# A hybrid RWKV-7 / sparse-attention layer on one core: block 1's weight sums of the feed-forward moved from accumulating transfers to VectorE, and the fp32r weight parts moved to other offsets

## The chip, the cores and the metric

One core of a Trainium2 chip runs the whole kernel. The metric is the device time of one execution in microseconds (us), as a median over runs. A profiled execution gives a trace beside it: when each instruction began on each engine, and what it waited for. The engines are PE (TensorE: matmuls, and PEld, its weight loads), DVE (VectorE), ACT (ScalarE), POOL (GpSimd) and SP (SyncE, which issues most of the DMA transfers here).

## What is computed

One layer for 512 tokens of width 1024 in float32. A normalised input is multiplied by one wide matrix `w_in`; its columns feed an RWKV-7 group (a recurrence, solved in chunks) and a sparse-attention group; both results go through `w_out`. Then comes the part that the change is mostly about, a SwiGLU feed-forward of inner width 2816, and a last norm:

```python
h = h + jnp.concatenate([y_r, y_n], axis=-1) @ w_out[l]
xn = rms_norm(h, norm_ffn[l])
h = h + (jax.nn.silu(xn @ w_gate[l]) * (xn @ w_up[l])) @ w_down[l]
return rms_norm(h, norm_final)
```

## The kernel before, in words

**Products in three matmuls.** A float32 product is made of fp32r parts: each operand is split into a high half (ACT copies it with rounding, L145) and a low half (DVE subtracts the high half from the value, L147). `mm3` (L163 to L166) then adds up three matmuls: high by high (L164), high by low (L165), low by high (L166). For each matmul PE loads a *stationary* operand of 128 columns and streams a *moving* operand of 256 or 512 columns past it; the load for the next matmul runs while the present one streams. L164 and L165 of a product differ in one operand only.

**Gate and up.** The 2816 inner columns are done in 11 blocks of 256 (`q` = 0 to 10). A block is a Strassen-like scheme: a 2 by 2 split of (w_gate, w_up) against a 2 by 2 split of the tokens takes seven products instead of eight, named by their weights: B11, B21, T2, T1, T3, B22, T4. Each product (`prod`) is 24 matmuls of 128x256: 2 halves of 128 columns, 4 blocks of the inner dimension, three matmuls each. The weights' parts are stationary; the tokens' parts (A11, A12, S1 to S4, A22) are made once, and move. Four raw quarters of a block come from memory: B11 and B21 (w_gate), B12 and B22 (w_up). The sums are T1 = B11 + B12, T2 = T1 + B22, T3 = B12 + B22 and T4 = T2 + B21.

**How the sums are made** (`class Weights`). `load_rest` issues on SP a plain transfer of B11 into the tile `t1` (L1154), of B22 into `b22` (L1155) and of B12 into `t3` (L1156). POOL then issues two transfers that *add* into what lies there: B12 onto `t1` (L1158) and B22 onto `t3` (L1159). So T1 and T3 come out of memory transfers, each a plain one and an adding one behind it. DVE makes T2 (L1163) and T4 (L1171). `put` splits each weight into its parts.

**Block 1 and the handover.** Blocks 0 and 1 are prepared while `w_out` is multiplied and the tokens' parts are made (`ffn_norm`). Block 0's sums are early. Block 1's `t1`, `t2` and `t3` lie in a tile of the tag `L`, which comes free only when the token parts have been made from the tile `raw` (last read at L1090 and L1114). The trace shows block 1's transfers as `L<-in_w_gate_dram` and `L<-in_w_up_dram`.

**The order of the work** is set by a scheduler at build time that places each engine's instructions in one fixed row, by its own estimate and by `tc.high_priority()`. Each engine works its row in order.

**Where the parts lie.** `parts` and `operand` cut the parts out of tiles that have 64 spare elements, from element `off` on (4 bytes each). The start addresses in a partition, mod 256, in the program as built: the tiles `whi` and `wlo` at 160; `L` (A11, A12, S3, A22; xh, xl) at 160; `gin` (S2) and `b8` (S4) at 32; `kB` (S1) at 64; the window operand `t4` of `job_cmp1` at 160. So a weight part in gate and up (off=56, 224 bytes) lies at 128, and a part that moves in the projections (off=8, 32 bytes; `moving` lists those jobs) at 192. Block 0's B11, B21, T2 and T1 lie in `b8` tiles without an offset.

Of the kernel before, what the change touches and what calls it, by code (L numbers as in the profile page):

```python
# [46 lines left out]
def hybrid_layer(ctx: ExitStack, tc: tile.TileContext, x, positions, norm_mix, w_in, mu_shift, w0, w2, a0, a2,  # L47
                 g2, k_k, k_a, r_k, lnx_w, lnx_b, pe_k, wk1, bk1, wk2, pe_v, wv1, bv1, wv2, w_out, norm_ffn,
                 w_gate, w_up, w_down, norm_final, out):
    nc = tc.nc  # L50
    PE, DVE, ACT, POOL = nc.tensor, nc.vector, nc.scalar, nc.gpsimd
# [12 lines left out]
    def st(shape, tag, bufs=1, dtype=F32):  # L64
        return sb.tile(list(shape), dtype, name=tag, tag=tag, bufs=SB_BUFS.get(tag, bufs))
# [3 lines left out]
    w_in, w_out, w_gate, w_up, w_down = (w.rearrange("l a b -> (l a) b") for w in (w_in, w_out, w_gate, w_up, w_down))  # L69
# [22 lines left out]
    raw0 = st([128, 2048], "wraw").rearrange("p (k n) -> p k n", n=256)  # L92
# [48 lines left out]
    def split(src, hi, lo, pool=False, lo_pool=False):  # L141
        if pool:
            POOL.tensor_copy(hi, src)
        else:
            ACT.activation(hi, src, AF.Copy)  # L145
        pool = pool or lo_pool
        (POOL if pool else DVE).tensor_sub(lo, src, hi.bitcast(F32))  # L147

    def parts(raw, tags=("whi", "wlo"), pool=False, lo_pool=False, off=0):

        b, n = raw.shape[1:]
        hi, lo = (st([128, 2048 + PAD], tag, 2, F32R) for tag in tags)
        v = [t[:, off:off + b * n].rearrange("p (k n) -> p k n", n=n) for t in (hi, lo)]
        with tc.high_priority():
            for k in range(0, b, max(b // 2, 1)):
                e = k + max(b // 2, 1)
                split(raw[:, k:e], v[0][:, k:e], v[1][:, k:e], pool, lo_pool)
        return v
# [58 lines left out]
    def proj_tok(w, t, m=1):  # L217

        n = w[0].shape[2]
        p = pj()  # L220
        for u in range(m):
            sl = slice((t + u) * 128, (t + u + 1) * 128)
            for k in range(KB):
                mm3(p[:, u * n:u * n + n], xh[:, k, sl], xl[:, k, sl], w[0][:, k], w[1][:, k], k == 0, k == KB - 1)
        return p[:, 0:m * n]
# [74 lines left out]
    for t in range(NT):  # L300
        next(norm)
        if t == 0:
            w0p = parts(raw0, off=8)
        ACT.activation(ctok[:, t].rearrange("p h d -> p (h d)"), proj_tok(w0p, t), AF.Copy)
    w1p = parts(raw1, lo_pool=True)
    pt = ps("s")
# [193 lines left out]
    def job_r(half):  # L500
        def f(w):
            if "rar" not in T:
                T["rar"] = st([128, 4, 2, S], "L")
            for j in range(2):
                i = half * 2 + j
                rx = st([128, S], "t2")
                mix(proj_tile(w, j * 128), i, rx)
                DVE.tensor_mul(ch(T["rar"][:, i, 1]), ch(rx), T["ep"][:, i, :, 1:65])
        return f
# [79 lines left out]
    def job_v(half):  # L589
        def f(w):  # L590
            if half == 0:
                T["rv"] = st([128, 4, S], "b8")
            for j in range(2):
                i = half * 2 + j
                mix(proj_tile(w, j * 128), 8 + i, T["rv"][:, i])
        return f
# [48 lines left out]
    def job_qs(half):  # L645
        def f(w):
            if half == 0:
                T["qtok"] = st([128, NT, 8, 64], "b8")
            for t in (0, 2):
                rotate(T["qtok"][:, t:t + 2, 4 * half:4 * half + 4], tok_pair(w, t), tab_pair(t), 0.125)  # L650
        return f
# [70 lines left out]
    def cols(c0, n=256):  # L722
        return lambda: load(w_in[:, c0:c0 + n], n)
# [11 lines left out]
    def load_kv(c):  # L735
        raw = st([128, 2048], "wraw").rearrange("p (k n) -> p k n", n=256)
        for b in range(2):
            c0 = kvw + 256 + c + 256 * b
            nc.sync.dma_start(raw[:, :, b * 128:b * 128 + 128], w_in[:, c0:c0 + 128].rearrange("(k p) n -> p k n", p=128))
        return raw  # L740

    mk, mv = cmp_jobs(wk1, 0), cmp_jobs(wv1, 1)
    def then(job, *fs):
        return job[0], lambda w: [f(w) if f is job[1] else f() for f in (job[1],) + fs]

    hk, hv = lambda: hidden(0, "bk1"), lambda: hidden(1, "bv1")
    jobs = [(None, job_lat), (load_tail, job_tail), (cols(1024), job_v(0)), mk[0], then((cols(1280), job_v(1)), gate), mk[1], then((cols(512), job_k(0)), hk), mv[0], (cols(768), job_k(1)), then(mv[1], hv), then((cols(0), job_r(0)), solve, compressed), (cols(256), job_r(1)), then((lambda: load_kv(128), job_vt), solve2), (lambda: load_kv(0), job_ks), then((cols(RCOLS), job_qs(0)), solve3, solve4), (cols(RCOLS + 256), job_qs(1))]

    moving = [jobs[i][1] for i in (3, 5, 7, 9, 12, 13, 14, 15)]
    raws, w = [jobs[1][0]()], w1p  # L750
    for n, (_, f) in enumerate(jobs):
        if n + 2 < len(jobs):
            raws.append(jobs[n + 2][0]())
        wn = parts(raws.pop(0), off=8 if jobs[n + 1][1] in moving else 0) if raws else None
        f(w)
        w = wn

# [187 lines left out]
    for t in range(NT):  # L945
        n = (t + 1) * 128
# [120 lines left out]
    def operand(tag, off=0):  # L1067
        v = st([128, 2048 + (PAD if tag in ("whi", "wlo") else 0)], tag, dtype=F32R)[:, off:off + 2048]
        v = v.rearrange("p (x k n) -> p x k n", x=2, n=256)
        return v[:, 0], v[:, 1]  # L1070
# [6 lines left out]
    def ffn_norm(src):  # L1077
        xn2 = st([128, 2, D], "b8")
        for t in range(NT):
# [36 lines left out]
                put("A22", a22)  # L1116
            yield

    turn2 = [0]

    class Weights:
# [12 lines left out]
        def put(self, name, v, tag=None):  # L1134
            if tag is None:
                tag = ("whi", "wlo")[turn2[0] % 2]
                turn2[0] += 1
            o = operand(tag, 56 if tag != "b8" else 0)
            split(v, *o)
            setattr(self, name, o)  # L1140

# [5 lines left out]
        def load_rest(self):  # L1147
            self.b22 = st([128, 2048], "wraw")[:, 0:1024].rearrange("p (k n) -> p k n", n=256)
            if self.q % 2:
                tt = st([128, 4, HK, 256], "L")  # L1150
                self.t1, self.t2, self.t3 = (tt[:, i] for i in range(3))
            else:
                self.t1, self.t2, self.t3 = (st([128, HK, 256], "t4") for _ in range(3))
            nc.sync.dma_start(self.t1, self.quarter(w_gate, 0))  # L1154
            nc.sync.dma_start(self.b22, self.quarter(w_up, 1))  # L1155
            nc.sync.dma_start(self.t3, self.quarter(w_up, 0))  # L1156
            with tc.high_priority():
                POOL.dma_start(self.t1, self.quarter(w_up, 0), accum_op=OP.add)  # L1158
                POOL.dma_start(self.t3, self.quarter(w_up, 1), accum_op=OP.add)  # L1159

        def middle(self, tag=None):
            with tc.high_priority():
                DVE.tensor_add(self.t2, self.t1, self.b22)  # L1163
                self.put("T2", self.t2, tag)
                self.put("T1", self.t1, tag)

        def end(self):
            with tc.high_priority():
                self.put("T3", self.t3)
                self.put("B22", self.b22)  # L1170
                DVE.tensor_add(self.t2, self.t2, self.b21)  # L1171
                self.put("T4", self.t2)
# [135 lines left out]
    for n, (a, b) in enumerate(GROUPS):  # L1308
        one, two = halves[n]
        a11, a21, a12, a22 = (h[:, :, x] for h in (one, two) for x in (left, right))  # L1310
        lead, end = n == 0, n == 1
        t1, t2 = block4(a, 0, "wraw"), block4(b, 1, ("gin", "kB")[n])
        t3 = st([128, 4, 512], "wraw") if lead else None
        t3 = [t3[:, 2 * i:2 * i + 2] if lead else st([128, 2, 512], "t4") for i in range(2)]
        for i in range(2):
            nc.sync.dma_start(t3[i], down(a, 1)[:, 2 * i:2 * i + 2])
        t2s.append(t2)
        DVE.tensor_sub(a21, a22, a21)
        multiply(m1, a_side(a11), b_side(t1), lead, end)
        DVE.tensor_add(a11, a21, a11)  # L1320
        with tc.high_priority():
            for i in range(2):
                h = slice(2 * i, 2 * i + 2)
                DVE.tensor_add(t1[:, h], t1[:, h], t3[i])
                POOL.dma_start(t3[i], down(b, 1)[:, h], accum_op=OP.add)
            DVE.tensor_add(t2, t2, t1)
        multiply(m5, a_side(a21), b_side(t1), lead, end)
        multiply(m6, a_side(a11), b_side(t2), lead, end)
        DVE.tensor_sub(a21, a11, a22)
        multiply(m7, a_side(a21), b_side(t3), lead, end)  # L1330
# [30 lines left out]
    for t, banks in accumulate(*jit(lambda k: hid[PLAIN[k]]), w_down, 6, None, [PLAIN[k] * 128 for k in (0, 2, 4)], held, rest):  # L1361
        xo, o = x2[:, t], o2[:, t % 2]
# [49 lines left out]
```

## Time and profile before

| | |
|---|---|
| median of 3 runs | 751.76 us (751.45 to 752.36) |
| the profiled execution, device time | 753.52 us |
| its span, first to last instruction | 751.5 us |
| PE / DVE / ACT / POOL busy | 720.7 / 592.5 / 399.6 / 165.1 us |
| mean granted TensorE clock | 0.979 |

The profiled execution took 1.76 us more than the median of the runs, and 2.0 us of it lie around the span. Times in the trace count from the span's start. A matmul's duration in the trace overlaps that of the next one, so what a matmul costs in a row of matmuls is read from start to start. The gate and up blocks stand between about 413 and 634 us; the `w_in` projections between 11 and 212 us; the down projection follows up to the end.

### The profile page before, as it was taken

Reading aid. Unit: us, or ns where it says so; the run is one execution under the profiler, and the core shown is the slowest. Engines: PE = TensorE matmul, PEld = TensorE weight load, DVE = VectorE, ACT = ScalarE, POOL = GpSimd, SP = SyncE. Lnnn points to the kernel's source line nnn. Section 1 sums busy time; section 2 is a strip of 40 time slices with the busy share of each in tenths; the row PEclk is TensorE's granted clock in tenths of the full one; section 3 lists DMA queues with packets and bytes.
Section 4 is the critical chain, followed back from the end, with each engine's and each line's share of the span. In section 5 each row is a group of like instructions: output and inputs, shape, how many; then the busy total and the mean of one; then the engine's idle time right before and its main releaser. Section 6 shows DMA issues by size and latency. Waiting matters only on the chain.

```text
span 751.5 us, 14937 instructions
## 1 busy us (share of the span) xinstructions
PE 720.7 (96%) x6045; PEld 630.3 (84%) x6045; DVE 592.5 (79%) x1089; ACT 399.6 (53%) x666; POOL 165.1 (22%) x262
## 2 busy tenths in 40 slices
PE   7999999998889999999999969999999999999996
PEld 6867887898778788767788969999999999877885
DVE  5488688879868888788358959869798899999835
ACT  6398735324367866757538535435444455465414
POOL 3210053038534452443000111111101101010000
PEclk8999999999989999999999979999999999999998
DMA  7723543100062000230320778887867719453302
GB/s 252 206 82 110 168 113 112 57 3 2 3 222 33 2 2 2 57 115 1 113 85 1 190 159 227 184 221 169 225 168 187 180 57 287 161 113 112 141 0 112
DMA packets 73466, 87.01 MB, mean 116 GB/s; under 512 B 4996, under 2 KB 62934, under 8 KB 73398
## 3 DMA queue, kind: packets, MB, share of 16 engines
q1 hardware_dynamic: 60694, 72.43, 29.4%
q0 software_dynamic: 12704, 13.63, 11.8%
q8 instruction: 47, 0.77, 0.4%
q14 instruction: 21, 0.17, 0.1%
HBM read 83.96 MB, written 2.10 MB: 115 GB/s over the span
## 4 chain that ended last, share of the span: by engine, by line
PE 66%; DVE 23%; DMA 5%; issue 3%; ACT 2%; POOL 0%; SPq 0%; DVEq 0%; ACTq 0%
PE ps_ra L166 6%; PE ps_ra L165 6%; PE ps_ra L164 6%; PE ps_pj L166 6%; PE ps_pj L164 5%; PE ps_pj L165 5%; PE ps_o L1006 3%; DVE wlo L147 3%; PE ps_s L166 3%; PE ps_s L164 3%; PE ps_s L165 3%; DMA L<-in_w_up_dram 3%; PE ps_pj L998 3%; DVE L L147 2%; DVE whi L147 2%
## 5 line engine op out<-in xcount | busy, mean ns | idle before, releaser
L145 ACT ACTIVATE whi<-wraw 128x1024 fp32r<-128x1024 f32 (+1 forms) x63 | 62.7, 1032 | 40.7 <-issue 11.7
L147 DVE TENSOR_TENSOR wlo<-wraw,whi 128x1024 fp32r<-128x1024 f32 (+1 forms) x46 | 58.4, 1295 | 15.6 <-ACT whi L145 12.1
L995 POOL TENSOR_SCALAR whi<-whi,m,gates 128x128 f32<-128x128 f32 (+3 forms) x64 | 42.5, 680 | 37.2 <-DVE m L993 28.7
L166 PE MATMUL ps_ra<-L,wlo 128*128 128x512 f32 (+2 forms) x136 | 48.0, 354 | 0.0
L165 PE MATMUL ps_pj<-L,whi 128*128 128x512 f32 (+1 forms) x128 | 45.2, 353 | 0.0
L164 PE MATMUL ps_pj<-L,whi 128*128 128x512 f32 (+1 forms) x128 | 44.8, 355 | 0.3 <-ACT whi L145 0.3
L165 PE MATMUL ps_ra<-L,whi 128*128 128x512 f32 (+2 forms) x128 | 44.1, 345 | 0.0
L166 PE MATMUL ps_pj<-L,wlo 128*128 128x512 f32 (+1 forms) x128 | 43.9, 343 | 0.1
L164 PE MATMUL ps_ra<-L,whi 128*128 128x512 f32 (+2 forms) x128 | 43.8, 344 | 0.0
L992 ACT ACTIVATE whi<-whi,m 128x128 f32<-128x128 f32 (+3 forms) x64 | 35.4, 554 | 9.6 <-DVE m L991 8.4
L164 PE MATMUL ps_ra<-whi,L 128*128 128x256 f32 (+1 forms) x108 | 34.4, 321 | 0.5 <-ACT L L145 0.5
L165 PE MATMUL ps_ra<-wlo,L 128*128 128x256 f32 (+1 forms) x108 | 34.5, 319 | 0.2 <-DVE wlo L147 0.2
L166 PE MATMUL ps_ra<-whi,L 128*128 128x256 f32 (+1 forms) x108 | 34.0, 316 | 0.0
L991 DVE CUSTOM_DVE_ANT_0 whi<-ps_s,negb 128x128 f32<-128x128 f32 (+3 forms) x64 | 29.3, 484 | 5.9 <-PE ps_pj L998 2.5
L166 PE MATMUL ps_pj<-whi,L 128*128 128x256 f32 (+1 forms) x108 | 33.8, 314 | 0.0
L165 PE MATMUL ps_pj<-wlo,L 128*128 128x256 f32 (+1 forms) x108 | 33.6, 312 | 0.0
L164 PE MATMUL ps_pj<-whi,L 128*128 128x256 f32 (+1 forms) x108 | 33.5, 313 | 0.0
L1158 POOL DMA_DIRECT2D t<-in_w_up_dram x6 | 8.0, 1332 | 97.6 <-DVE b L1090 58.0
L166 PEld LDWEIGHTS ps_ra<-L,wlo 128*128 128x128 f32 (+1 forms) x136 | 25.1, 185 | 4.0 <-issue 0.5
L166 PEld LDWEIGHTS ps_pj<-L,wlo 128*128 128x128 f32 x128 | 24.5, 191 | 3.7 <-DVE wlo L147 0.9
L164 PEld LDWEIGHTS ps_pj<-L,whi 128*128 128x128 f32 x128 | 24.4, 190 | 3.8 <-ACT whi L145 0.8
L165 PEld LDWEIGHTS ps_pj<-L,whi 128*128 128x128 f32 x128 | 24.4, 190 | 3.5 <-DVE L L147 0.4
(706 smaller groups left out, 2562.4 us busy)
## 6 DMA issues: line engine op xcount, KB each, us to landing
wraw<-in_w_gate_dram SPq DMA_DIRECT2D x22, 512.0 KB
wraw<-in_w_in_dram SPq DMA_DIRECT2D x9, 1024.0 KB
wraw<-in_w_down_dram SPq DMA_DIRECT2D x9, 1024.0 KB
t<-in_w_up_dram POOLq DMA_DIRECT2D x12, 512.0 KB, 6.5
wraw<-in_w_up_dram SPq DMA_DIRECT2D x11, 512.0 KB
L<-in_w_up_dram POOLq DMA_DIRECT2D x10, 512.0 KB, 6.0
wraw<-in_w_out_dram SPq DMA_DIRECT2D x4, 1024.0 KB
wraw<-in_w_in_dram SPq DMA_DIRECT2D x6, 512.0 KB
```

The lines of the kernel that those rows point to most:

```text
L145: ACT.activation(hi, src, AF.Copy)
L147: (POOL if pool else DVE).tensor_sub(lo, src, hi.bitcast(F32))
L164: PE.matmul(o, lh, rh, start=start, stop=False)
L165: PE.matmul(o, lh, rl, start=False, stop=False)
L166: PE.matmul(o, ll, rh, start=False, stop=stop)
L991: DVE.tensor_tensor_reduce(pr[:, i], pS[:, i], negb[:, S - n:S], scale=-1.0, scalar=3e38, op0=OP.add, op1=OP.min, accum_out=m[:, i, 0:1])
L992: ACT.activation(pr[:, i], pr[:, i], AF.Exp, scale=-1.0, bias=m[:, i, 0:1], accum_out=m[:, i, 1:2])
L995: POOL.tensor_scalar(pr[:, i], pr[:, i], m[:, i, 2:3], gv[:, 1 + b0 + i, h:h + 1], op0=OP.mult, op1=OP.mult)
L998: PE.transpose(pT[:, j], prr[:, x, j * 128:j * 128 + 128], ident)
L1006: PE.matmul(po[q, 2 * g:2 * g + 2], vtok[:, j % (t + 1), b0 + j // (t + 1), g], pTs[:, par, j], start=False, stop=g == 1 and bs[-1] == 1 a ...
L1158: POOL.dma_start(self.t1, self.quarter(w_up, 0), accum_op=OP.add)
```

## The change

Two things, in one diff:

1. For block 1 alone (`self.q == 1`) SP issues two plain transfers only: B12 into `t3` and B22 into `b22`. The plain transfer of B11 into `t1` and both adding transfers are gone. DVE makes T1 from the raw B11 (which is in SBUF for its own product anyway) and `t3`, then T2 as before, and T3 as `t3 + b22`.
2. The parts of weights get other offsets. In gate and up the offset depends on the product (`SHIFT`, elements), in the projections' moving weights it is 48 elements in place of 8.

```diff
@@ main loop over t (projection of the first columns)
-            w0p = parts(raw0, off=8)
+            w0p = parts(raw0, off=48)
@@ loop over jobs
-        wn = parts(raws.pop(0), off=8 if jobs[n + 1][1] in moving else 0) if raws else None
+        wn = parts(raws.pop(0), off=48 if jobs[n + 1][1] in moving else 0) if raws else None
@@ before class Weights
+    SHIFT = {"B11": 16, "B21": 16, "T2": 48, "T1": 56, "T3": 16, "B22": 48, "T4": 16}
@@ put
-            o = operand(tag, 56 if tag != "b8" else 0)
+            o = operand(tag, SHIFT[name] if tag != "b8" else 0)
@@ load_rest
+            if self.q == 1:
+                nc.sync.dma_start(self.t3, self.quarter(w_up, 0))
+                nc.sync.dma_start(self.b22, self.quarter(w_up, 1))
+                return
             nc.sync.dma_start(self.t1, self.quarter(w_gate, 0))
@@ middle
+                if self.q == 1:
+                    DVE.tensor_add(self.t1, self.b11, self.t3)
                 DVE.tensor_add(self.t2, self.t1, self.b22)
@@ end
+                if self.q == 1:
+                    DVE.tensor_add(self.t3, self.t3, self.b22)
                 self.put("T3", self.t3)
```

What the offsets do to the distance from the moving operand's start to the stationary operand's start (stationary minus moving, mod 256 bytes):

| matmuls of 128x256 | how many | before | with the change |
|---|---|---|---|
| gate and up, B11 B21 T3 T4 on A11 A12 S3 A22 | 1008 | 224 | 64 |
| gate and up, T2 on S2, B22 on S4 | 504 | 96 | 64 |
| gate and up, T1 on S1 | 240 | 64 | 64 |
| block 0's parts in `b8` (T1, T2, B11, B21) | 96 | 224, 0, 128 | the same |
| projections and `job_cmp1` with moving weights | 544 | 224 | 64 |

The 128x512 matmuls keep their distance. "192 bytes apart" in the change's own words is the same distance counted the other way round.

The scheduler also orders the instructions around the handover from block 0 to block 1 anew. The names in the rows: `whi` and `wlo` are the tiles of the weights' parts (T1 in `whi`, T2 and T3 in `wlo`), `t_4814`, `t_4924` and `lora` hold block 0's partial results, `L` stands for block 1's sums.

DVE before, from block 0's last split on (L1163 makes T2, the first L147 behind it T1's low half):

```order
L147 TENSOR_TENSOR whi<-t_4553,whi 128x1024
L1231 TENSOR_TENSOR t_4924<-ps_s,t_4814 128x512
L1234 TENSOR_TENSOR t_4814<-ps_pj,t_4814 128x512
L1235 TENSOR_TENSOR lora<-ps_pj,t_4924 128x512
L1238 TENSOR_TENSOR t_4924<-ps_ra,t_4924 128x512
L1239 SCALAR_TENSOR_TENSOR b_4813<-t_4924,t_4815 128x2x256
L1163 TENSOR_TENSOR L<-L,wraw 128x1024
L147 TENSOR_TENSOR whi<-L,whi 128x1024
```

DVE with the change, from the same split on (L1170 makes T1, L1178 T3, L1171 T2; L1241, L1244, L1245 are the former L1231, L1234, L1235):

```order
L147 TENSOR_TENSOR whi<-t_4553,whi 128x1024
L1170 TENSOR_TENSOR L<-wraw,L 128x1024
L1241 TENSOR_TENSOR t_4924<-ps_s,t_4814 128x512
L1178 TENSOR_TENSOR L<-L,wraw 128x1024
L1171 TENSOR_TENSOR L<-L,wraw 128x1024
L1244 TENSOR_TENSOR t_4814<-ps_pj,t_4814 128x512
L1245 TENSOR_TENSOR lora<-ps_pj,t_4924 128x512
L147 TENSOR_TENSOR whi<-L,whi 128x1024
L1252 TENSOR_TENSOR t_4814<-ps_s,t_4814 128x512
L147 TENSOR_TENSOR wlo<-L,wlo 128x1024
```

All three sums of block 1 now stand ahead of T1's split, and T3's sum, which reads `b22`, stands ahead of T2's.

PE with the change, at the same handover (the first row is block 0's last matmul; before, all 24 matmuls of T1, `ps_ra<-kB,whi`, followed it in one piece):

```order
L166 MATMUL ps_s<-L,whi 128x256
L164 MATMUL ps_ra<-kB,whi 128x256
L165 MATMUL ps_ra<-kB,whi 128x256
L164 MATMUL ps_pj<-gin,wlo 128x256
L165 MATMUL ps_pj<-gin,wlo 128x256
L164 MATMUL ps_s<-L,wlo 128x256
L165 MATMUL ps_s<-L,wlo 128x256
L166 MATMUL ps_ra<-kB,whi 128x256
```

Two matmuls each of T1, T2 and T3 that need the high halves alone now stand ahead of the first one that needs T1's low half.

## Rows read from the trace of the kernel before

**Rows 1.** The page: the span; busy time, share and instructions by engine; the granted TensorE clock in 40 slices (tenths); the chain of waits by engine.
```profile
span 751.5 us, 14937 instructions
PE 720.7 (96%) x6045; PEld 630.3 (84%) x6045; DVE 592.5 (79%) x1089; ACT 399.6 (53%) x666; POOL 165.1 (22%) x262
PEclk8999999999989999999999979999999999999998
PE 66%; DVE 23%; DMA 5%; issue 3%; ACT 2%; POOL 0%; SPq 0%; DVEq 0%; ACTq 0%
```

**Rows 2.** Busy time by window. Columns: window in us, its length, busy us (instructions) of PE, PEld, DVE, ACT, POOL, then granted TensorE clock, DMA share, GB/s. The handover in two windows, a long stretch of gate and up, one block (from one product's start to the same product's start in the next block), and the last three blocks.
```profile
433.80:439.79 5.99, 0.01 (x1) 0.00 (x0) 1.19 (x2) 1.10 (x2) 0.90 (x1) 0.72 0.61 117
439.79:446.34 6.55, 6.08 (x26) 5.79 (x27) 5.17 (x7) 3.66 (x5) 1.68 (x2) 0.50 0.77 160
446.72:575.34 128.62, 128.62 (x1104) 128.62 (x1103) 107.99 (x121) 57.50 (x64) 16.83 (x13) 1.00 0.83 201
499.68:519.25 19.57, 19.57 (x171) 19.57 (x169) 15.17 (x19) 8.96 (x10) 2.60 (x3) 1.00 0.88 188
575.34:634.00 58.66, 58.66 (x505) 58.66 (x505) 52.86 (x56) 29.61 (x33) 6.29 (x5) 1.00 0.60 162
```

**Rows 3.** The chain of waits in order of time, at the handover: start us, us, what.
```profile
427.46 11.12 DMA L<-in_w_up_dram
438.60 1.22 DVE L L1163
439.83 1.18 DVE whi L147
441.05 0.58 PE ps_ra L166
```

**Rows 4.** PE's instructions in order of time at the handover: start us, us, engine, line, operation, out<-in, shape, count, [idle before, and what ended it].
```profile
433.53 0.28 PE L166 MATMUL ps_s<-L,whi 128*128 128x256 f32 x1
439.79 0.58 PE L164 MATMUL ps_ra<-kB,whi 128*128 128x256 f32 x1 [5.98 <-ACT whi L145]
441.05 0.58 PE L166 MATMUL ps_ra<-kB,whi 128*128 128x256 f32 x1 [0.46 <-DVE whi L147]
...
446.34 0.42 PE L164 MATMUL ps_pj<-b,whi 128*128 128x256 f32 x1
```

**Rows 5.** DVE's and ACT's instructions in order of time ahead of and at the handover, columns as in rows 4.
```profile
422.99 1.22 DVE L1171 TENSOR_TENSOR t<-t,wraw 128x1024 f32<-128x1024 f32 x1
424.13 1.21 DVE L147 TENSOR_TENSOR whi<-t,whi 128x1024 fp32r<-128x1024 f32 x1
...
426.40 0.68 DVE L1228 TENSOR_TENSOR t<-ps_ra,t 128x512 f32<-128x512 f32 x1
427.00 1.21 DVE L147 TENSOR_TENSOR whi<-t,whi 128x1024 fp32r<-128x1024 f32 x1
428.13 0.68 DVE L1231 TENSOR_TENSOR t<-ps_s,t 128x512 f32<-128x512 f32 x1
...
438.69 1.06 ACT L145 ACTIVATE whi<-L 128x1024 fp32r<-128x1024 f32 x1 [13.38 <-DMA L<-in_w_up_dram]
439.77 1.23 DVE L147 TENSOR_TENSOR whi<-L,whi 128x1024 fp32r<-128x1024 f32 x1
```

**Rows 6.** The DMA issues of SP and POOL ahead of the handover, in order of time, columns as in rows 4 (the last SP row is block 2's).
```profile
423.10 0.37 SPq L1154 DMA_DIRECT2D L<-in_w_gate_dram  x1
424.24 0.37 SPq L1155 DMA_DIRECT2D wraw<-in_w_up_dram  x1
...
426.92 0.61 SPq L1131 DMA_DIRECT2D wraw<-in_w_gate_dram  x1
427.46 1.30 POOL L1158 DMA_DIRECT2D L<-in_w_up_dram  x1 [9.85 <-DVE t L1228]
```

**Rows 7.** What SP's queue waited for between 423 and 433 us: line and releaser, us in total, times, longest.
```profile
SPq L1155 <- DMA wraw<-in_w_up_dram: 5.0, 1, 5.0
```

**Rows 8.** PE's instructions in order of time, columns as in rows 4: in block 0 the third matmul of the product T1 on S1 (`kB,b`), the start of T2 on S2 (`gin,b`), its third matmul and the start of the next product; then the first matmuls of five products of a later block (T2 on S2 `gin`, T1 on S1 `kB`, T3 on S3 `L`, B22 on S4 `b`, T4 on A22 `L`).
```profile
419.55 0.28 PE L166 MATMUL ps_s<-kB,b 128*128 128x256 f32 x1
422.15 0.28 PE L164 MATMUL ps_ra<-gin,b 128*128 128x256 f32 x1
422.56 0.28 PE L166 MATMUL ps_ra<-gin,b 128*128 128x256 f32 x1
425.19 0.28 PE L164 MATMUL ps_pj<-L,whi 128*128 128x256 f32 x1
...
502.48 0.28 PE L164 MATMUL ps_pj<-gin,whi 128*128 128x256 f32 x1
505.30 0.28 PE L164 MATMUL ps_ra<-kB,wlo 128*128 128x256 f32 x1
508.02 0.28 PE L164 MATMUL ps_s<-L,whi 128*128 128x256 f32 x1
510.82 0.28 PE L164 MATMUL ps_pj<-b,wlo 128*128 128x256 f32 x1
513.65 0.28 PE L164 MATMUL ps_ra<-L,whi 128*128 128x256 f32 x1
```

**Rows 9.** The chain of waits in the last blocks of gate and up: start us, us, what.
```profile
576.52 8.02 DMA L<-in_w_up_dram
...
604.70 4.89 DMA wraw<-in_w_down_dram
```

**Rows 10.** Busy time by window, columns as in rows 2: the projections with moving weights, ahead of and beside the solve of the recurrence.
```profile
143.00:157.40 14.40, 14.40 (x256) 13.60 (x257) 9.93 (x15) 2.75 (x4) 0.00 (x0) 1.00 0.01 1
157.40:204.00 46.60, 41.24 (x507) 39.06 (x495) 45.14 (x117) 16.46 (x31) 32.51 (x70) 1.00 0.01 2
```

## The prediction

> **What bounds the kernel now.** I read the page first: PE is busy 720.7 of 751.5 us and makes up two thirds of the chain that ended last [rows 1]. So a change pays where PE stands still or where a matmul gets shorter. The clock's slices show a dip a little past the middle [rows 1]; the windows resolve it. From 433.80 to 439.79 us PE does nothing, and from 439.79 to 446.34 its granted clock is 0.50, that is 1.2 GHz in place of 2.4 [rows 2]. Before it fell PE had stood still since 433.7. Then the chain of waits tells why: an accumulating transfer of w_up, issued at 427.46, holds it for 11.12 us, and only then DVE sums and splits, and PE goes on [rows 3]. This is T1 of block 1, the handover from block 0. Behind it, from 446.72 to 575.34, PE is busy throughout at full clock, while DVE works 108 of 128.6 us [rows 2]: there the spacing of matmuls sets the time. After about 575 the chain runs through DMA landings and DVE though PE is still busy [rows 2, 9].
>
> **A. The handover.** Removed: one plain transfer and two accumulating ones of 512 KB, with POOL's two issues; POOL has one block's fewer in its row, which no other work waits for. Added: two DVE sums of 128x1024. From start to start such a DVE step takes 1.14 us (422.99 to 424.13), one of 128x512 takes 0.60 (426.40 to 427.00) [rows 5]. The new row of DVE, begun where the old one stands, goes: block 0's last split at 427.00, T1's sum 428.13, L1241 at 429.27, T3's sum 429.87, T2's sum 431.01, L1244 432.15, L1245 432.75, T1's low half from 433.35, done at 434.6 (1.23 us [rows 5]). ACT makes T1's high half by about 430.4 and those of T3 and T2 by 433.3 to 434.3 (1.06 each [rows 5]; it is idle until 438.69 now). PE's last matmul of block 0 starts at 433.53 [rows 4], so it could go on at 433.65. It has six matmuls that need high halves alone, 0.7 us, up to 434.3. The new wait is 0.2 to 0.3 us, on T1's low half.
>
> This holds if `t3` is there by 428.1 and `b22` by 429.9. `t3` now takes the first place in SP's row, issued at 423.10; the transfer that has that place today was down by 427.46, when POOL added to it [rows 6]. `b22` is issued at 424.24, third of three, and SP's queue waited 5.0 us for it, from some 427.5 to 432.5 [rows 6, 7]. With 4.4 us from issue to landing, as for the first, it would be there at 428.6. It is second now, so I put it at 430 and the wait at 0.5 us. What is queued behind T3's sum on DVE while it waits for `b22` is all of block 1: T2's sum, two adds that free PSUM, and T1's low half.
>
> In numbers: between 433.65 and the start of the 27th matmul at 446.34 lie 12.69 us and 26 matmuls [rows 2, 4]. At 0.1135 us each (below) they need 2.95, with the wait 3.45. **Gain 9.2 us.** No wait at all gives 9.7. With `b22` at 432.5 T1's low half comes 1.14 + 1.14 + 0.60 + 0.60 + 1.23 = 4.7 us later, at 437.2; six matmuls are gone by then, 20 follow in 2.3, and the gain is 6.8. What covers the two sums is DVE's own idle time, 5.91 of the 6 us ahead of T2's old sum (433.8 to 439.79: busy 1.19 [rows 2]); without that cover they would cost 2.3 us.
>
> **B. Spacing of the matmuls in gate and up.** A product is 24 equal matmuls. From start to start T1 on `kB` takes 2.72 us, T2 on `gin` 2.82, T3 on `L` 2.80, B22 on `b` 2.83 [rows 8]. In bytes from the moving to the stationary operand these lie 64, 96, 224 and 96 apart. That it is the distance and not the tile `kB` is seen in block 0: there `kB` meets a part at a distance of 224, and 22 matmuls from the third on take 419.55 to 422.15, 118 ns each, against 2.72/24 = 113; `gin` at a distance of 0 takes 422.56 to 425.19, 120 ns [rows 8]. The change brings all to 64. I price a product at 2.72: four of 2.80, one of 2.82 and one of 2.83 give up 4 x 0.08 + 0.10 + 0.11 = 0.53 us per block of 19.57 [rows 2, 8]. The stretch 446.72 to 575.34 is 6.57 blocks: 3.5 us. The last three blocks could give 1.6 more, but the end of that stretch hangs on DMA and DVE [rows 2, 9]; I count 0.5. **Gain 4.0 us**, between 0 (the distance is a coincidence) and 5.1.
>
> The Trainium skill (TensorE: Matmul & The Clock Gate, section on what each phase is for) gives PE two independent SBUF read ports and says that loading the next weights "doesn't steal SBUF read bandwidth from the running matmul". By that rule a distance between the two operands changes nothing and B and C are 0. The rows disagree: the same tile, engine and shape takes 118 or 113 ns [rows 8].
>
> DVE has 15.2 us of work in a block [rows 2], so a block of 19.04 does not starve it. Steps that are only moved (SP's row moves up by one transfer, the offsets of ACT's and DVE's operands) I price at nothing: the next plain transfers have over 10 us until use, and DVE's 128x1024 steps take 1.21 to 1.23 us at offsets with and without shift [rows 5]. The range of C covers them.
>
> **C. The projections with moving weights.** 480 matmuls and 64 of the compression go from distance 224 to 64, 3.4 ns each, 1.9 us if PE set the time everywhere. The first 96 wait for the norm. In 143.00 to 157.40 PE is busy all the time; in 157.40 to 204.00 DVE is, 45.14 of 46.60 [rows 10], and PE's gain is lost there. **Gain 0.5 us**, between 0 and 1.5.
>
> **The sum.** 9.2 + 4.0 + 0.5 = 13.7 us. The profiled execution took 753.52 us, so its like would take 739.8; the median of the runs stands 1.76 below it, and 751.76 - 13.7 gives **738.1 us**. The best of all bounds is 9.7 + 5.1 + 1.5 = 16.3, 735.5 us.
>
> **Rivals.**
> *The distance sets nothing* (the skill's rule, or the shorter product has another cause in block 1 to 10, say what DVE and ACT do beside it): A alone, 751.76 - 9.2 = 742.6 us. For it: the differences are 3 to 4 ns in 117. Against: block 0's comparison within one tile.
> *A shorter wait takes the place of the old one*: `b22` lands as late as today, since one transfer's landing is that of its last part, and DVE's row stands still in front of T3's sum. Gain of A 6.8, time 740.5 us; if the clock falls in those 3 us of idling, up to 3 us more. For it: `b22` took 8.3 us today [rows 6, 7]. Against: one transfer fewer ahead of it, and no accumulating ones beside it.
> *Slower*: the same place, DVE's wait in front of T3's sum, gone wrong. T1's low half follows `b22` by 4.7 us, and if PE idles so long that its clock falls as today, the 20 matmuls behind take 4.4 us (0.22 each: from 441.05 to 446.34 there are 24 [rows 2, 4]). Break-even with 446.34 is a landing at 437.2; to undo B and C as well it has to come after 441.7, 17 us after its issue. At 444 us the time is 754. The longest transfer here took 11.12 [rows 3], so this is far off.
> *It does not do what it says*: the addresses and the instruction rows leave no doubt on the sums, so only the first rival remains of this.
>
> **How the numbers follow.** The forecast has 0.64; the distance without effect 0.14; the late `b22` 0.13; both of these together, 745 us, 0.03, all faster; both with a fallen clock and A almost gone 0.03; slower 0.03. The range takes the forecast with its bounds, the late `b22` and the first rival: 735.4 to 743.2. So faster by over 0.2% (1.5 us, about what a measurement of this kernel can tell from no change) has 0.94, within it 0.03, slower by more 0.03.
>
> **What would show it right or wrong.** In the profile after: no window at the handover with PE idle for over 1 us, and no stretch at 0.50 of the clock there (A); the chain of waits without `L<-in_w_up_dram` in that place. Starts of products 2.72 us apart on every tile and a block of 19.05 us (B); if `L` products still take 2.80, the distance was not it. A block of 19.05 with the end not earlier by B's sum means that the gain is lost in the down projection, where DVE's row is full. If DVE shows an idle time in front of T3's sum that a landing ended, the second rival holds.

## The result, and the profile after

The changed kernel took **747.99 us** (median of 4 runs; 747.73 to 749.5) beside 751.61 us of the kernel before in the same set, a ratio of 0.9938 [0.991, 0.9966]. It is faster, but by 3.6 us and not by 13.7; 747.99 lies above the range of 735.4 to 743.2. In a second set it took 747.9 us, ratio 0.9921 [0.9895, 0.9946].

The kernel before gave 751.61, 756.3, 753.76 and 752.35 us in the four sets, and the start of any program varies by some 4 us in the traces. So I compare kernels of one set by their medians, and traces from a common mark on: one matmul of block 0, ahead of the handover (429.77 us before, 431.79 after; the 3901st matmul of the program). From it to the last matmul's start the kernel before needs 314.8 us, the changed one 309.0, in its second trace 307.7.

The page of the changed kernel, lines as in [rows 1]:

```profile
span 747.8 us, 14927 instructions
PE 718.9 (96%) x6045; PEld 627.9 (84%) x6045; DVE 593.0 (79%) x1091; ACT 398.3 (53%) x666; POOL 162.2 (22%) x260
PEclk7999999999989999999999999999999999999999
PE 64%; DVE 22%; DMA 7%; issue 3%; ACT 2%; POOL 0%; SPq 0%; DVEq 0%; ACTq 0%; POOLq 0%
```

The dip of the clock past the middle is gone, yet DMA's share of the chain has risen from 5 to 7%. Busy time by window, columns as in [rows 2]: the handover's first 31 matmuls and what follows them, the long stretch of gate and up, the blocks 3, 4 and 6 (each from the start of its T2 product to the next block's), the last three, and a piece of the down projection, the latter of the changed kernel and, in the last line, of the kernel before:

```profile
435.67:439.31 3.64, 3.63 (x31) 3.42 (x29) 3.64 (x5) 2.15 (x3) 0.00 (x0) 1.00 0.95 141
439.31:446.70 7.39, 7.39 (x66) 7.39 (x65) 7.39 (x9) 3.19 (x3) 0.00 (x0) 1.00 0.55 172
446.70:575.34 128.64, 126.78 (x1095) 126.37 (x1095) 107.27 (x122) 58.01 (x66) 18.12 (x14) 1.00 0.81 198
474.97:494.29 19.32, 19.32 (x171) 19.32 (x170) 15.82 (x19) 8.85 (x10) 3.88 (x3) 1.00 0.96 245
494.29:514.49 20.20, 19.80 (x171) 19.59 (x169) 14.37 (x18) 8.73 (x10) 2.59 (x2) 1.00 0.74 154
533.79:555.05 21.26, 19.80 (x170) 19.59 (x169) 14.37 (x18) 8.73 (x10) 2.59 (x2) 1.00 0.73 147
575.34:634.00 58.66, 58.51 (x479) 57.19 (x478) 50.41 (x55) 27.22 (x31) 4.99 (x4) 1.00 0.63 165
634.00:660.00 26.00, 23.92 (x104) 18.88 (x103) 26.00 (x23) 13.78 (x14) 2.40 (x2) 1.00 0.50 151
...
634.00:660.00 26.00, 26.00 (x117) 21.42 (x116) 26.00 (x26) 14.14 (x15) 2.29 (x2) 1.00 0.56 167
```

The handover runs at full clock. Block 3 is shorter than 19.57 us; blocks 4 and 6 are longer, by a stall of 0.40 and 1.46 us and by a longer busy time (19.80). In 634 to 660 DVE has no idle time at all, as before, and PE loses 2.08 us there that it did not lose before.

PE at the handover, columns as in [rows 4]:

```profile
435.67 0.28 PE L164 MATMUL ps_ra<-kB,whi 128*128 128x256 f32 x1
...
436.32 0.38 PE L164 MATMUL ps_s<-L,wlo 128*128 128x256 f32 x1
...
436.66 0.34 PE L166 MATMUL ps_ra<-kB,whi 128*128 128x256 f32 x1
...
439.07 0.28 PE L165 MATMUL ps_ra<-kB,whi 128*128 128x256 f32 x1
```

435.67 is the first matmul behind block 0 and 439.07 the 27th: 3.40 us for what took 12.69. DVE beside it, answering [rows 5]:

```profile
430.14 1.22 DVE L1170 TENSOR_TENSOR L<-wraw,L 128x1024 f32<-128x1024 f32 x1
...
431.88 1.21 DVE L1178 TENSOR_TENSOR L<-L,wraw 128x1024 f32<-128x1024 f32 x1
433.01 1.22 DVE L1171 TENSOR_TENSOR L<-L,wraw 128x1024 f32<-128x1024 f32 x1
...
435.35 1.21 DVE L147 TENSOR_TENSOR whi<-L,whi 128x1024 fp32r<-128x1024 f32 x1
```

No row has an idle time behind it: DVE waits for no landing. T2's sum, the third of the rows, will matter below: it starts 1.2 us behind the mark, where it started 8.8 behind it before (438.60 [rows 3]).

Five products of block 3, answering [rows 8] (T2 on `gin`, T1 on `kB`, T3 on `L`, B22 on `b`, T4 on `L`):

```profile
474.97 0.28 PE L164 MATMUL ps_s<-gin,wlo 128*128 128x256 f32 x1
...
477.80 0.28 PE L164 MATMUL ps_pj<-kB,whi 128*128 128x256 f32 x1
...
480.55 0.28 PE L164 MATMUL ps_ra<-L,wlo 128*128 128x256 f32 x1
...
483.27 0.28 PE L164 MATMUL ps_s<-b,whi 128*128 128x256 f32 x1
...
486.10 0.28 PE L164 MATMUL ps_pj<-L,wlo 128*128 128x256 f32 x1
```

2.83, 2.75, 2.72 and 2.83 us at one and the same distance: here only the products on `L` became shorter.

What DVE waited for between 446 and 640 us (us in total, times, longest), first of the kernel before, then of the changed one:

```profile
DVE L L1163 <- DMA L<-in_w_up_dram: 6.8, 2, 3.6
DVE L L1163 <- DMA wraw<-in_w_up_dram: 3.1, 1, 3.1
DVE t L1163 <- DMA wraw<-in_w_up_dram: 3.0, 4, 1.2
```
```profile
DVE L L1171 <- DMA L<-in_w_up_dram: 19.3, 4, 6.9
DVE t L1171 <- DMA wraw<-in_w_up_dram: 6.4, 4, 2.8
```

All lines are T2's sum; its tile is called `L` in odd blocks and `t` in even ones. The waits in odd blocks have doubled, from 9.9 to 19.3 us, those for an adding transfer have nearly tripled. The chain of waits shows how (blocks 7 to 9: start, us, what):

```profile
530.86 10.05 DMA L<-in_w_up_dram
540.93 1.23 DVE L L1171
542.16 0.60 DVE t L1228
542.76 1.15 DVE wlo L147
...
553.96 3.58 DMA wraw<-in_w_up_dram
557.63 1.23 DVE t L1171
...
561.19 1.15 DVE wlo L147
...
562.36 8.94 DMA L<-in_w_gate_dram
...
571.98 8.20 DMA L<-in_w_up_dram
580.20 1.23 DVE L L1171
```

T2's sum of block 7 (540.93) waits for an adding transfer. Behind it in DVE's row stands the low half of B22 of block 6 (542.76), and PE waits for that:

```profile
542.21 0.28 PE L165 MATMUL ps_s<-b,wlo 128*128 128x256 f32 x1
543.95 0.39 PE L166 MATMUL ps_s<-b,wlo 128*128 128x256 f32 x1 [1.46 <-DVE wlo L147]
```

Then block 8's `b22` (3.58 us) holds T2's sum of block 8, behind which stands the last split of block 7 (561.19), which frees `L` for block 9: a plain transfer (8.94), an adding one (8.20), T2's sum of block 9. It is a loop over two blocks, 39.3 us long, 20.7 of them in three transfers. PE stands in it too: from 543.95 to 553.92 the chain runs over its matmuls, and between T2's sums of blocks 5 and 7 from 503.38 to 528.53. PE alone would need 2 x 19.32 = 38.6.

One more row stands behind these waits. From 451.94 to 512.64 eight adding transfers follow each other on POOL without a break, each but the first issued 0.31 us after the landing of the one ahead (landed 492.42, next issued 492.73); T2's sum of block 5 (500.37) waits for one of them. That row alone is not the limit, though: the kernel with the sums in all odd blocks (experiment 3) has pauses of 4.8 and 11.1 us in it, and its T2's sums of blocks 3 and 5 lie 40.2 us apart, against 40.0 here.

Followed matmul by matmul from the mark, PE of the changed kernel is 9.4 us ahead of the kernel before behind the handover (matmul 3961), 10.2 at matmul 4497 in block 4, 8.3 near the end of gate and up (5501), and 5.8 from matmul 5701, in the down projection, to the end. In its second trace it is 9.5, 10.3, 8.6 and 7.1. So some 2 us go in the blocks, and 2.6 and 1.6 in the down projection.

### The profile page after: what moved, and what is told of

Its sections match the earlier page's. It is cut to its first block, busy times and chain, and to the rows that moved or that the text cites. A ratio compares the mean times of both kernels' runs of the same rounds, so it can differ in the third digit from the quotient of the medians.

```text
span 747.8 us, 14927 instructions
## 1 busy us (share of the span) xinstructions
PE 718.9 (96%) x6045; PEld 627.9 (84%) x6045; DVE 593.0 (79%) x1091; ACT 398.3 (53%) x666; POOL 162.2 (22%) x260
## 4 chain that ended last, share of the span: by engine, by line
PE 64%; DVE 22%; DMA 7%; issue 3%; ACT 2%; POOL 0%; SPq 0%; DVEq 0%; ACTq 0%; POOLq 0%
PE ps_ra L165 6%; PE ps_ra L166 6%; PE ps_ra L164 6%; PE ps_pj L166 5%; PE ps_pj L164 5%; PE ps_pj L165 5%; DMA L<-in_w_up_dram 3%; DVE wlo L147 3%; PE ps_o L1006 3%; PE ps_s L164 3%; PE ps_s L166 3%; PE ps_s L165 3%; PE ps_pj L998 3%; DVE L L147 2%; PE ps_s L985 1%
## 5 line engine op out<-in xcount | busy, mean ns | idle before, releaser
L147 DVE TENSOR_TENSOR wlo<-wraw,whi 128x1024 fp32r<-128x1024 f32 (+1 forms) x46 | 58.4, 1296 | 15.6 <-ACT whi L145 12.1
L164 PE MATMUL ps_ra<-whi,L 128*128 128x256 f32 (+1 forms) x108 | 35.3, 329 | 0.3 <-ACT L L145 0.3
L166 PE MATMUL ps_ra<-whi,L 128*128 128x256 f32 (+1 forms) x108 | 34.9, 325 | 0.0
L164 PEld LDWEIGHTS ps_pj<-L,whi 128*128 128x128 f32 x128 | 24.1, 188 | 4.9 <-DVE t L1248 1.2
L166 PE MATMUL ps_s<-L,whi 128*128 128x256 f32 (+1 forms) x88 | 26.3, 300 | 1.3 <-DVE whi L147 1.3
```

What stands on the lines that cost most here:

```text
L164: PE.matmul(o, lh, rh, start=start, stop=False)
L166: PE.matmul(o, ll, rh, start=False, stop=stop)
```

## The experiments

In the table the mark is the matmul named above; "T2 (1)" and "T2 (9)" are the starts of T2's sums of blocks 1 and 9, all read from one trace of each kernel, in us.

| kernel | median | mark to T2 (1) | T2 (1) to T2 (9) | T2 (9) to last matmul | mark to last matmul |
|---|---|---|---|---|---|
| before | 751.61 to 756.3 | 8.8 | 146.0 | 160.0 | 314.8 |
| changed (first, second trace) | 747.99, 747.9 | 1.2, 1.2 | 147.2, 146.9 | 160.6, 159.6 | 309.0, 307.7 |
| sums alone (first, second trace) | 747.98, 748.25 | 1.2, 1.2 | 147.5, 147.9 | 159.9, 159.7 | 308.7, 308.8 |
| offsets alone | 754.43 | 8.5 | 146.8 | 159.8 | 315.2 |
| sums in odd blocks | 746.94 | 1.2 | 147.7 | 160.0 | 308.9 |
| T1's sum in odd blocks | 749.88 | 1.8 | 148.3 | 159.9 | 310.0 |
| `b22` in `L` | 751.67 | 1.2 | 146.4 | 165.7 | 313.4 |
| both: `b22` in `L`, sums in odd blocks | 743.43, 744.05 | 1.2, 1.2 | 137.5, 137.7 | 165.8, 167.1 | 304.5, 306.0 |
| the same, old offsets | 745.85 | 1.2 | 136.0 | 169.9 | 307.2 |

**1. Each part alone.** The sums without the offsets (`off=8`, 56 for every product), then the offsets without the sums.

> The sums of block 1 on VectorE alone, the weights' parts at their old offsets. Theory L (from block 2 on the loop of transfers sets the pace: T4's split frees L, plain load of T1, accumulating transfer, T2's sum; the end follows T2's sum of block 9 by a fixed row of VectorE): 748.0 us +- 0.7, as with both parts, L products at 2.80 us, and fewer or no stalls of PE in the B22 products. Rival P (what PE saves adds up at the end): 748.0 + 10 blocks x 0.26 us = 750.6 us.

> The new offsets alone, block 1 with its three plain and two accumulating transfers. L: block 9's T1 transfer lands no earlier than before by more than 1 us, 750.8 to 751.6 us. P: 751.6 - 2.6 - 0.5 = 748.5 us. Both: some products at 2.72 and some at 2.83 us on one and the same tile, and the handover as before, with PE idle for 6 us and a stretch at 0.50 of the clock.

Sums alone: 747.98 us (before in this set 756.3; ratio 0.9888 [0.9849, 0.9926]). The forecasts stand for the first set, where the kernel before took 751.61, so the time alone does not decide between them. From the mark on the kernel needs 308.7 us, the changed one 309.0: its gain is the whole gain, as L says, and experiment 2 shows it within one set. PE stalls less before the down projection, as L also says: once, 0.76 us, against 0.40, 1.46 and 0.15 us. Offsets alone: 754.43, ratio 0.9973 [0.9951, 0.9995], less than P's 3.1 us. The medians differ by 1.9, but from the mark on its one trace is 0.4 us longer than before's, T2's sum of block 9 coming no earlier; so nothing gained in gate and up reaches the end, and where the 1.9 come from these runs do not show.

**2. The change and the sums alone, side by side.** Their instruction rows are the same on every engine; only addresses differ.

> The changed kernel once more, beside the one with the sums alone on the same chip. Theory E (the end follows T2's sum of block 9 by 160 us, whatever PE saves before it): T2's sum of block 9 at 147 +- 1.5 us behind that of block 1, the end 160 +- 1 us behind it, and the time equal to that of the sums alone within 0.7 us. Rival P (shorter matmuls add up): 2.5 us below the sums alone.

> The sums alone once more; its instruction rows are those of the changed kernel on every engine, only operands' addresses differ. E: equal to the changed kernel within 0.7 us, with PE's stalls in gate and up shorter by what its matmuls are longer. P: 2.5 us above it.

747.9 and 748.25 us (ratios to before 0.9921 [0.9895, 0.9946] and 0.9928 [0.9904, 0.9953]): 0.35 us apart, within E's 0.7 and far from P's 2.5. At matmul 5501 PE is 8.3 and 8.6 us ahead with the offsets and 7.5 and 7.3 without, at the last one 5.8 and 7.1 against 6.1 and 6.0. So some 1 us of the shorter matmuls is there at the end of gate and up, and little or nothing of it at the end. In the table the last matmul starts 160 us behind T2's sum of block 9, within 0.6, in all kernels whose `b22` is where it was; from 634 to 680 DVE's row is full (46.00 of 46 us in the changed kernel), and what PE brings along is lost there.

**3. Taking the adding transfers out of the odd blocks.** First both sums on DVE, then T1's alone.

```diff
-            if self.q == 1:                   # in load_rest, middle and end
+            if self.q in (1, 3, 5, 7, 9):
```
```diff
+            if self.q in (3, 5, 7, 9):        # load_rest: t3 and b22 plain, as block 1
...
+                if self.q in (3, 5, 7, 9):    # middle, behind T1's sum
+                    POOL.dma_start(self.t3, self.quarter(w_up, 1), accum_op=OP.add)
```

> Both parts of the change, and T1's and T3's sums on VectorE in blocks 3, 5, 7 and 9 too: no accumulating transfer into L at all, 8 sums of 1.14 us more on VectorE. L: T2's sum of block 9 no longer waits for a landing and comes 8 to 12 us earlier than in the kernel before, the end 742.5 us (740 to 745.5). P (VectorE's or PE's work sets the pace, the landings only look late): 748 us, or up to 9 us more if VectorE is full: 748 to 757.

> As the one with sums in all odd blocks, but in blocks 3, 5, 7 and 9 only T1's sum is on VectorE (4 sums more); T3's second part is still added by an accumulating transfer, issued once T1's sum has read the tile. L: 743 us (740.5 to 746), since T3 is used a product or two later than T2; if its landing is late now, PE stalls in front of T3's product instead. P: 748 to 752.

746.94 (ratio 0.9887 [0.9835, 0.9939]) and 749.88 us (0.9896 [0.9843, 0.995]; its runs lie from 744.14 to 751.1). Theory L's numbers, 742.5 and 743, both failed; 749.88 lies in P's 748 to 752, and 746.94 is no better than the sums of block 1 alone in this set (0.9888). T2's sum of block 9 itself waits for no landing any more and still comes 147.7 us behind that of block 1: T1's sum, which now stands ahead of it in DVE's row, waits 5.27 us for the plain transfer into `L` (L1171, the row below the chain). The chain of the kernel with both sums shows why:

```profile
531.29 3.77 DMA wraw<-in_w_up_dram
...
536.23 1.22 DVE L L1172
...
549.24 4.05 DMA wraw<-in_w_up_dram
...
553.38 1.23 DVE t L1172
...
558.12 9.21 DMA L<-in_w_up_dram
...
577.86 1.14 DVE L L1172
```
```profile
567.42 1.23 DVE L1171 TENSOR_TENSOR L<-wraw,L 128x1024 f32<-128x1024 f32 x1 [5.27 <-DMA L<-in_w_up_dram]
```

Three transfers still stand one behind the other, here with no matmul of PE between them. One is gone from `L`, but `b22` of the odd block now stands in the loop too: it goes into a `wraw` buffer that only T4's sum of the block before frees. So not one late transfer but the loop through buffers holds the pace.

**4. Taking `b22` of the odd blocks out of `wraw`.** The tile `L` has four quarters, of which three were used.

```diff
             if self.q % 2:
                 tt = st([128, 4, HK, 256], "L")
-                self.t1, self.t2, self.t3 = (tt[:, i] for i in range(3))
+                self.t1, self.t2, self.t3, self.b22 = (tt[:, i] for i in range(4))
```

> The changed kernel, but b22 of the odd blocks lies in the unused fourth quarter of the tile L and not in a wraw buffer. Theory W (the pace from block 3 on is a loop of VectorE's row and of transfers that wait for buffers; in the odd blocks of the changed kernel its last link is the accumulating transfer into L): 747 to 748.3 us, since that link stays, and the even blocks' wait for b22 (0.9 to 2.9 us) gets shorter. Rival D (VectorE's own work is the pace, the waits only fill it): no change, 748.

> As the one with T1's and T3's sums on VectorE in all odd blocks, with b22 of the odd blocks in the fourth quarter of L. W: a loop of two blocks loses one transfer of 4 us into wraw, and runs at PE's 38.6 us instead of 40.3: T2's sum of block 9 is 144 us behind that of block 1 instead of 147.7, the end 743.5 us (742 to 745.5). D: as with wraw, 746.9, T2's sum of block 9 at 147.7 behind that of block 1.

With the sums of experiment 3 it gave 743.43 us (ratio 0.9876 [0.9836, 0.9917]), W's number; D fell. That the number fits so well is luck: T2's sum of block 9 comes 137.5 us behind that of block 1, 6.5 less than W's 144, and the end follows it by 165.8 in place of 160. From block 3 to 5 and from 5 to 7 T2's sum now takes 34.0 and 37.0 us, less than PE's 38.6, so DVE gets ahead of PE (then 40.8 to block 9). It makes the sum of block 9 without a wait:

```profile
568.27 1.22 DVE L1179 TENSOR_TENSOR L<-L 128x1024 f32<-128x1024 f32 x1
569.41 1.22 DVE L1172 TENSOR_TENSOR L<-L 128x1024 f32<-128x1024 f32 x1
```

And PE is busy for all of the long stretch (columns as in [rows 2]):

```profile
446.70:575.34 128.64, 128.64 (x1117) 128.64 (x1116) 113.64 (x129) 59.56 (x67) 9.04 (x7) 1.00 0.59 158
```

`b22` in `L` alone was a miss for W and D: 751.67 us (ratio 0.9966 [0.994, 0.9993]), 3.8 above the changed kernel of the same set. Its issues in front of T2's sum of block 3, and the windows (columns as in [rows 2]):

```profile
447.63 0.37 SPq L1160 DMA_DIRECT2D L<-in_w_gate_dram  x1
448.04 0.50 SPq L1161 DMA_DIRECT2D L<-in_w_up_dram  x1
...
452.02 1.29 POOL L1164 DMA_DIRECT2D L<-in_w_up_dram  x1 [14.91 <-DVE t L1245]
```
```profile
446.00:452.00 6.00, 6.00 (x54) 6.00 (x53) 6.00 (x8) 3.03 (x4) 0.00 (x0) 1.00 1.01 337
458.00:462.70 4.70, 4.70 (x43) 4.70 (x42) 0.00 (x0) 1.06 (x1) 0.00 (x0) 1.00 1.12 321
```

The DMA engines are full, T2's sum starts at 462.73, 5.9 us after DVE was free, and every odd block still waits for its adding transfer (19.0 us in four). Its row of DVE behind block 9 is another one, too (165.7 us to the end). Freeing one link of the loop did not help while the adding transfers stayed.

**5. The price of spacing and of the handover where nothing holds PE back.**

> The kernel with the sums on VectorE and b22 in L in all odd blocks, again, to stand beside the next two on one chip: 743.4 us +- 1.5.

> The same kernel and the same instruction rows, with the weights' parts at their old offsets. Theory E2 (spacing counts once PE and not the loop of transfers sets the end): 2.80 in place of 2.76 us a product on the average, 0.26 us a block, 8 blocks from the third on: 2.1 us above it, 745.5. Rival Z (spacing never reaches the end): 743.4, equal within 0.7.

> The same kernel, but block 1 as in the kernel before: three plain and two accumulating transfers, b22 in wraw. It prices the handover where the later blocks hold nothing back. E2: 743.4 + 9.2 = 752.6 us, the whole loss of PE's. Rival C (VectorE, which works ahead of PE from block 2 on, catches part of it up, so that less than the stall counts): 743.4 + 6 = 749.4 us.

744.05 us (ratio 0.9894 [0.9861, 0.9927]) and, with the old offsets and the same instruction rows, 745.85 (0.9917 [0.9892, 0.9943]): 1.8 us apart, E2 expected 2.1, Z nothing. The intervals overlap, and from the mark on the two traces differ by 1.1 us only, so this favours E2 without proving it. The windows of block 5 agree with it, new offsets first:

```profile
511.27:530.58 19.31, 19.31 (x170) 19.31 (x169) 17.33 (x20) 9.49 (x11) 0.00 (x0) 1.00 0.47 132
```
```profile
515.99:535.56 19.57, 19.57 (x170) 19.57 (x169) 17.46 (x21) 9.09 (x11) 0.00 (x0) 1.00 0.41 122
```

The kernel with the old block 1 gave 756.57 us (1.0066 [1.0041, 1.0092]), 12.5 above. That is more than either theory. Between the traces from the mark on lie 9.7 us at the end: some 6.5 behind the handover, 11.2 at the end of gate and up, by new waits of PE for low halves in later blocks, which the scheduler ordered anew, and 1.5 less again in the down projection. It does not price the handover cleanly.

**6. Other distances.** `(SHIFT[name] + 8 * (self.q - 1)) % 64`.

> The changed kernel with the weights' parts shifted by a further 32 bytes from block to block, so that every product meets eight distances. Theory M (the distance alone sets the spacing): one duration for each distance on all tiles, 113 to 114 ns at 64 from moving to next stationary operand, 117 to 120 at the others. Rival N (at one distance there are two durations, a whole product keeps one of them, and its first matmuls decide): 113 and 118 both occur at 64, and at other distances too.

N holds at 64: in block 9, which lies at that distance, the matmuls on `L` and `kB` start 113 to 115 ns apart on the mean of each line of `mm3`, those on `gin` and `b8` 117 to 118. The means at the other seven distances lie between 116 and 122 (119 to 120 at 0, 117 to 119 at 192). So 64 is the only distance of the eight with the short spacing, but it does not secure it; N's two durations at other distances did not show. Each other distance was met in one or two blocks of one trace. The single run took 748.07 us.

## Why the prediction was wrong

**A, the handover, held on PE.** I forecast no fall of the clock, `b22` at 430 and 3.45 us for 26 matmuls; they took 3.40, and PE gained 9.29 us against 9.2. `b22` was there at 430.9, which is 428.9 on the clock of the kernel before, since the mark stands 2.02 us later. So neither the 0.5 us wait nor the rival of a late `b22` came; T1's low half began at 435.35, that is 433.33, as the row said. That 3.40 meets 3.45 is in part luck: no wait for `b22`, but six matmuls took 0.99 us in place of 0.7, and the 20 behind them 2.41 in place of 2.27. One reading was loose: DVE's 5.91 us of idle time lie ahead of 438.60, and in 433.80 to 439.79 it was idle for 4.80; nothing hangs on it.

**The step that failed** is the sum's silent one: that what PE gains at the handover reaches the end. It rested on "so a block of 19.04 does not starve it" and on pricing the moved steps "at nothing", since "the next plain transfers have over 10 us until use". I counted DVE's work in a block (15.2 us) against the block's length, but DVE's work was not the limit: from block 3 to block 9 the loop of DVE's row and transfers that wait for buffers, with PE's matmuls between them, took 39.9 and 40.2 us for two blocks on the mean in the two traces. Before it took 39.6, where PE needed 39.14. The kernel before had two limits of nearly the same length. The table shows the account: T2's sum of block 1 comes 7.6 us earlier, not 9.3 (the rest lies behind that sum, where PE's matmuls ran at half clock); from there to block 9 it takes 0.9 to 1.2 us longer; and the end stays 160 us behind it. 7.6 - 1.2 - 0.6 = 5.8 us in the first trace, 7.6 - 0.9 + 0.4 = 7.1 in the second; the medians say 3.6 and 5.9. That T2's sum sets the end stood in [rows 9]: its chain begins with the adding transfer of block 9. I used that row only to cut B's end, and not to ask what A would be worth there. The last sign of the prediction named the down projection, where DVE's row is full, for B alone; of A's gain, too, some 1.4 us went there (both traces of the sums alone).

**B was half in size and next to nothing in effect.** It failed in its price of 2.72 us for every product at a distance of 64. A block without a stall takes 19.32 us, 0.25 less instead of 0.53, because in block 3 the products on `gin` and `b` kept 2.83 and the one on `kB` rose to 2.75; and a block with a stall loses more, since the products on `L` behind it take 2.83 again. The rival that the distance sets nothing is wrong as well. Over eight distances a matmul on `L` takes 113 to 114 ns at 64 and 119 to 120 at 0 (experiment 6). The Trainium skill (TensorE: Matmul & The Clock Gate, section "Step-by-step: what each phase is for") has the load of the next weights take no read bandwidth from the running matmul. By that rule the distance would set nothing, and these runs disagree with it, 113 to 114 ns against 119 to 120; whether it is the load that takes the time they do not show. But the time of the changed kernel holds little or nothing of B (experiment 2); of 4.0 us forecast, 1.8 appear between the medians and 1.1 between the traces once the loop is opened (experiment 5).

**C:** the same matmuls between 143.0 and 157.4 us took 14.37 us in the four traces with the old offsets there (before, sums alone twice, old offsets in experiment 5), and 14.22 to 14.25 in ten with the new: 0.14 us of the 0.5. The matmuls from 157.4 to 204 took 46.8 to 47.7 with the old offsets and with the new, so no gain shows there.

Opening the loop (experiment 4) gives 743.4 to 744.1 us, faster than both kernels here. In its two traces PE is 9.5 and 9.4 us ahead of the kernel before behind the handover and 10.3 and 8.8 at the last matmul, so there a gain of A's size reaches the end.

## What to carry to other kernels

A stall that is removed is worth no more than the slack of the next limit: before counting it at the end, follow a mark of every other loop (here one sum per block on DVE) from the stall to the end, and see whether it would come earlier. An engine's busy share says little of a loop in which it stands still for buffers, and taking one link out of such a loop may gain nothing or cost time, as `b22` in `L` alone did. A difference that is real in each instruction has to be tested in time with the same instruction rows.

## What was not expected of the hardware

Two spacings occur at one distance. At 64 bytes a whole product of 24 matmuls keeps 113 to 114 ns or 118 ns, and goes from one to the other at a product's boundary or a stall: after the stall behind 542.21 us the three products on `L` took 2.83 us each, where nothing stalled 2.72 to 2.74. Behind such a stall the next product on `gin` took 2.75 and that on `kB` 2.83 (from 555.05), the other way round than in block 3. What decides was not settled.

An adding transfer of 512 KB took 5.83 us where the next plain one was issued 2.7 us behind it (issued at 541.22 in the changed kernel) and 10.05 where plain ones were issued 0.4 us ahead of and 0.7 behind it (530.86).
